# A hybrid decoder layer on one core: timed step lists against a list scheduler, and the middle down stages in two seven-product blocks

## The chip, the core and the metric

The kernel runs on one core of a Trainium2 chip. The metric is device time in microseconds (us) for one execution; smaller is better. Three runs of the kernel before gave 1723.19, 1723.62 and 1724.95 us, so its median is 1723.62 us.

## The reference

One decoder layer over 256 tokens of width 2048, all in float32:

```python
x = x + 0.5 * swiglu_ffn(rms_norm(x, ffn1_norm), w_gate, w_up, w_down)   # 2048 -> 5632 -> 2048
z = rms_norm(x, mix_norm) @ w_in
...
x = x + y @ w_out
x = x + 0.5 * swiglu_ffn(rms_norm(x, ffn2_norm), ...)
return rms_norm(x, final_norm)

def swiglu_ffn(x, w_gate, w_up, w_down):
    return (silu(x @ w_gate) * (x @ w_up)) @ w_down
```

The change touches the two feed-forward networks (FFN1 and FFN2, tags 1 and 2 in the kernel). The mixer between them (a gated recurrence and a short convolution) is left as it is.

## The kernel before

**Numbers in two parts.** Every float32 operand is split into a high part (rounded to the fp32r type, a cast on ScalarE) and a low part (the rest, a subtraction on VectorE). A product is three matmuls per block of 128 rows: high by high, low by high, high by low. A *unit* is 512 rows (four blocks) of a weight matrix by 512 columns, 1 MB: loading one issues a transfer on SyncE's queue into a *raw* tile, then two ScalarE casts of 1024 elements give the high part, then one VectorE subtraction of 2048 elements gives the low part, and both go to one of the *pair* tiles. One unit against 128 tokens is 4 x 3 = 12 matmuls, with the activations stationary and 512 weight columns moving. There are two token tiles (t = 0, 1) of 128 tokens.

**Seven products for eight.** `seven` (L471) takes two units of rows and two groups of columns as a 2 x 2 block matrix against two token tiles and two units of activations. Instead of eight unit products it makes seven, of sums and differences of weights (w11, w12, w21, w22, summed in place on VectorE and once by an accumulating transfer on GpSimd's queue) and of activations (`seven_of`). Products are named p0 to p6, banks of PSUM a, c, d, e. Other units of the same columns are multiplied plainly (x01, x11, x00, x10: unit 0 or 1, column group 1 or 0). Some banks are copied out in between ("snaps" s1, s5, u2, u3) and added at the end by VectorE.

**The stages of an FFN.** Hidden columns come in eleven units of 512. After the first unit and a first pair of seven-product blocks comes a *down* stage: the product of the hidden units that are there with their rows of `w_down`, all 2048 output columns (`down`, L884). Then, for s = 1 and s = 3, a *fine* stage of four seven-product blocks (gate, up, gate, up; two column groups each, so four hidden units) and again a down stage. The down stage after s = 1 has hidden units 3 to 6 and is called the middle one here; the one after s = 3 has units 7 to 10 and is the last. The row lists of the fine blocks hold five 128-row blocks per product (`tall`, L844) and three per plain unit (`short`): 7 x 15 + 4 x 18 = 177 matmuls per block.

**A down stage before.** `product` (L400) makes columns 0 plainly from four units, then `seven` makes columns 2 and 1 from the two newest units m, n as seven products and the two others plainly, then `product` makes columns 3. The newest hidden units are transposed on TensorE in `settle`/`turn_hidden` (L593 to 619); each gives a high part (ScalarE), a low part (VectorE), and for the middle stage also an exact copy (ScalarE) from which the sums for the seven products are made.

**What orders the work.** Inside a fine stage the order of every engine is written out by hand: `block` (L1036) holds a list of (time, step) pairs (L1109 to 1157), `fine_blocks` (L1163) shifts them by 40.2 us per block, sorts them and traces them in that order with `Engine.pinned` set, which ties each instruction behind the one traced before it on its engine. Down stages are not pinned: there the framework may issue an instruction earlier than its place in the text when its data are there. SyncE's queue is in order of the text. `prepare` (L1198) makes small vectors for the mixer: two transposes on TensorE (`turns`), copies of their results and some twenty tiny steps on VectorE, and two activations on ScalarE. Before, `down` calls it in the middle down stage of FFN1, ahead of `seven` (L955).

Of the kernel before, what the change touches and what calls it, by code (L numbers as in the profile page):

```python
# [16 lines left out]
P = 128  # L17
# [30 lines left out]

@with_exitstack
def hybrid_block(ctx: ExitStack, tc: tile.TileContext, a: dict, out: bass.AP):  # L50
# [30 lines left out]
    psum = ctx.enter_context(tc.tile_pool(name="psum", bufs=8, space=bass.MemoryType.PSUM))  # L81

# [97 lines left out]
    plan = deque()  # L180
    opened = []

    def pool_of(name, side, bufs=1):
# [3 lines left out]
        "three": (["pair0", "pair1", "pair2"], ["raw2", "raw1", "raw0", "kept", "spare"]),  # L187
# [4 lines left out]
    def open_stage(layout, raws=None):  # L192
# [3 lines left out]
        for side, names in (("left", left), ("right", right)):  # L196
            for name in names:
                pools[name] = pool_of(f"{name}_{n}", side, 2 if name in ("kept", "spare") else 1)
# [13 lines left out]

    def least_recent(kind):
        i = plan.popleft() if kind == "pair" and plan else recent[kind][0]
        recent[kind].remove(i)
        recent[kind].append(i)
        return f"{kind}{i}"

    def raw_tile(name, rows, role=None):
        if role in ("kept0", "kept1") and not fine():  # L220
            if extra:
                return bigs.tile([P, rows, CW], F32, tag="big", name=f"raw_{name}")
            return pools["kept"].tile([P, rows, CW], F32, tag="kept", name=f"raw_{name}", bufs=2)
# [353 lines left out]
    def ffn(tag, norm, after, opening=False):  # L577
        with tc.tile_pool(name=f"ffn{tag}", bufs=1, side="left", reuse_waits="tile") as fp:
# [14 lines left out]
            def turn_hidden(u, t, h, again):  # L593
# [4 lines left out]
                for j in range(UK):  # L598
                    pe.transpose(pt[:, j * P : (j + 1) * P], h[:, j * P : (j + 1) * P], ident)
# [284 lines left out]
            def down(last):  # L884
                us = sorted(set(hidden) | {w[0] for w in waiting})
                m, n = us[-2:]
# [22 lines left out]
                for c in (0, 3):  # L909
                    if c == 3:  # L910
                        plan.extend([1, 0, 1, 2][4 - len(us) :])
                    end = last and tag == 2 and c == NC_D - 1
                    ps = product(
                        wd, c, us[:-2] + [n, m], hidden.get, f"d{tag}_{m}_{c}", end,
# [9 lines left out]
                    if c == 0:  # L924
                        sh = {}
                        two, last_sum, high, low = seven_of(
# [28 lines left out]
                        if tag == 1 and m == 5:  # L955
                            prepare()
                        seven(
                            wd, (whole(m), whole(n)), (2 * CW, CW), sh, [of_unit(u, hidden[u]) for u in us[:-2]],
# [77 lines left out]
            def block(w, cs, name, b, done, gating, follows, handed):  # L1036

                raw, parts, bank_of, snaps, rest = {}, {}, {}, {}, {}
                home = {
                    "w11": (tall[0], 0, f"kept{b % 2}"), "w12": (tall[0], 1, f"kept{1 - b % 2}"),  # L1040
                    "w21": (tall[1], 0, "tall2"), "w22": (tall[1], 1, "tall1"),
                    "x01": (short[0][0], 1, "short0"), "x11": (short[1][0], 1, "short1"),
# [29 lines left out]
                def to(n):  # L1072
                    if n not in bank_of:
                        bank_of[n] = bank(f"ps_{name}_{n}")
# [607 lines left out]
```

## Time and profile before

| | us |
|---|---|
| median of three runs | 1723.62 |
| the profiled execution | 1727.47 |
| its span (first to last instruction) | 1725.5 |
| TensorE busy | 1708.7 |
| VectorE busy | 1506.8 |
| ScalarE busy | 1093.3 |
| fine stages of FFN1, from 200.76 and from 449.85 | 163.20, 163.60 |
| fine stages of FFN2, from 1211.64 and from 1462.44 | 165.33, 165.08 |
| middle down stages, from 363.96 and from 1376.97 | 85.89, 85.47 |
| last down stage of FFN2, from 1627.52 to the last matmul | 89.48 |

How to read it: in the profile PE is TensorE's matmul side, PEld its weight loads, DVE VectorE, ACT ScalarE, POOL GpSimd, SP SyncE. Nearly all instructions carry line L43, that of a helper that records them, so groups are told apart by the names of their tiles: `raw_d` is a raw tile of `w_down`, `hi_d_p` and `lo_d_p` the parts of a seven-product operand, `hi_d_x` those of a plain unit beside it, `hi_d` those of `product`; `g` and `u` stand for gate and up. A matmul's recorded duration overlaps the next one's, so the distance from one start to the next is its real price.

### The profile page before, as it was taken

To read this page: it belongs to the slowest core of one execution; us is meant where nothing else is said; L and a number is where in the kernel's file an instruction comes from. 1 tells how busy PE (TensorE), PEld (TensorE's weight loads), DVE (VectorE), ACT (ScalarE), POOL (GpSimd) and SP (SyncE) were. 2 spreads that over 40 slices of the span, in tenths; PEclk is the share of its full clock that TensorE was granted. 3 is DMA by queue.
4 is the path that set the end of the run, shared out by engine and by line. 5 is a ranking of instruction groups with operands and counts; after the bars stand their busy time and mean duration, and the time that the engine had idled before them with its cause. 6 is when DMAs were issued, how large, how long until landed. Compare 5 with 4: busy or idle time off the path is not lost.

```text
span 1725.5 us, 20385 instructions
## 1 busy us (share of the span) xinstructions
PE 1708.7 (99%) x7937; PEld 1424.3 (83%) x7937; DVE 1506.8 (87%) x1290; ACT 1093.3 (63%) x1344; POOL 45.7 (3%) x78
## 2 busy tenths in 40 slices
PE   9999999999999999999999999999999999999998
PEld 8888888888888888888888888888788888788876
DVE  7989899988799977887997888889899887899886
ACT  7766566655576666666866666655666654666654
POOL 0100000000000000000000000000000000000000
PEclk9999999999999999999999999999999999999999
DMA  8765877775887665655556574665977656877653
GB/s 304 234 222 179 270 236 233 227 236 167 263 269 224 202 224 193 222 190 176 173 194 225 190 266 149 219 226 186 300 240 226 213 173 239 258 232 238 231 165 122
DMA packets 181583, 376.78 MB, mean 218 GB/s; under 512 B 7412, under 2 KB 10352, under 8 KB 177776
## 3 DMA queue, kind: packets, MB, share of 16 engines
q1 hardware_dynamic: 174656, 340.81, 56.4%
q0 software_dynamic: 6656, 33.63, 10.4%
q8 instruction: 62, 1.02, 0.2%
q10 hardware_dynamic: 176, 1.06, 0.2%
q14 instruction: 33, 0.27, 0.0%
HBM read 339.82 MB, written 2.10 MB: 198 GB/s over the span
## 4 chain that ended last, share of the span: by engine, by line
PE 77%; issue 5%; DMA 5%; DVE 2%; ACT 1%; SPq 0%; POOL 0%; DVEq 0%; POOLq 0%; ACTq 0%
PE ps_in L43 10%; PE ps_u_a L43 9%; PE ps_d L43 8%; PE ps_g_a L43 8%; PE ps_u_c L43 6%; PE ps_g_c L43 4%; PE ps_u_d L43 4%; PE ps_g_d L43 4%; PE ps_d_a L43 4%; PE ps_o L43 3%; DMA raw_g_w<-raw_g_w 2%; PE ps_d_c L43 2%; PE ps_u_e L43 2%; PE ps_d_d L43 2%; PE ps_g_e L43 2%
## 5 line engine op out<-in xcount | busy, mean ns | idle before, releaser
L43 ACT CAST hi_g_p<-raw_g_w 128x1024 fp32r<-128x1024 f32 x112 | 137.9, 1262 | 69.5 <-PE ps_g_a L43 16.4
L43 ACT CAST hi_u_p<-raw_u_w 128x1024 fp32r<-128x1024 f32 x112 | 137.8, 1261 | 62.0 <-PE ps_u_a L43 20.9
L43 DVE TENSOR_TENSOR lo_g_p<-raw_g_w,hi_g_p 128x2560 fp32r<-128x2560 f32 (+2 forms) x72 | 158.5, 2225 | 20.5 <-PE ps_d L43 14.3
L43 DVE TENSOR_TENSOR lo_u_p<-raw_u_w,hi_u_p 128x2560 fp32r<-128x2560 f32 (+2 forms) x72 | 158.9, 2226 | 11.1 <-ACT hi_u_p L43 10.1
L43 PE MATMUL ps_d<-hi_d,h 128*128 128x512 f32 x696 | 166.1, 390 | 0.0
L43 PEld LDWEIGHTS ps_d<-hi_d,h 128*128 128x128 f32 x696 | 130.0, 188 | 26.7
L43 ACT CAST hi_d<-raw_d 128x1024 fp32r<-128x1024 f32 x88 | 87.4, 1047 | 72.5 <-PE ps_d_d L43 23.6
L43 PE MATMUL ps_in<-xT_nm,hi_in 128*128 128x512 f32 x512 | 122.5, 391 | 0.0
L43 DVE TENSOR_TENSOR lo_d<-raw_d,hi_d 128x2048 fp32r<-128x2048 f32 x44 | 99.7, 2288 | 23.8 <-ACT hi_d L43 23.7
L43 PEld LDWEIGHTS ps_in<-xT_nm,hi_in 128*128 128x128 f32 x512 | 94.0, 188 | 18.8 <-ACT tha L43 0.5
L43 ACT CAST hi_d_p<-raw_d 128x1024 fp32r<-128x1024 f32 x84 | 84.8, 1047 | 35.5 <-DVE raw_d L43 24.8
L43 DVE TENSOR_TENSOR lo_d_p<-raw_d,hi_d_p 128x2048 fp32r<-128x2048 f32 x42 | 95.0, 2284 | 7.4 <-ACT hi_d_p L43 7.4
L43 DVE TENSOR_TENSOR lo_in<-raw_in,hi_in 128x2048 fp32r<-128x2048 f32 x32 | 73.2, 2287 | 21.1 <-ACT hi_in L43 20.7
L43 PE MATMUL ps_d<-lo_d,h 128*128 128x512 f32 x348 | 86.2, 389 | 0.0
L43 ACT CAST hi_in<-raw_in 128x1024 fp32r<-128x1024 f32 x64 | 64.2, 1048 | 33.4 <-PE ps_in L43 18.0
L43 PEld LDWEIGHTS ps_d<-lo_d,h 128*128 128x128 f32 x348 | 65.3, 188 | 13.6
L43 DVE TENSOR_TENSOR raw_g_w<-raw_g_w,raw_g_w 128x1024 f32<-128x1024 f32 (+2 forms) x40 | 68.8, 1753 | 8.6 <-DMA raw_g_w<-in_ffn_w_gate_dram 8.2
L43 DVE TENSOR_TENSOR raw_u_w<-raw_u_w,raw_u_w 128x1024 f32<-128x1024 f32 (+2 forms) x40 | 68.8, 1753 | 0.6
L43 PEld LDWEIGHTS ps_in<-xT_nm,lo_in 128*128 128x128 f32 x512 | 65.6, 191 | 2.5
L43 PE MATMUL ps_in<-xT_nm,lo_in 128*128 128x256 f32 x512 | 66.4, 283 | 0.0
L43 ACT CAST hi_g_x<-raw_g_x 128x1536 fp32r<-128x1536 f32 x32 | 47.2, 1474 | 21.6 <-DMA raw_g_x<-in_ffn_w_gate_dram 20.3
L43 PE MATMUL ps_u_a<-hi_u_p,x 128*128 128x512 f32 x224 | 57.5, 393 | 0.0
(503 smaller groups left out, 3956.7 us busy)
## 6 DMA issues: line engine op xcount, KB each, us to landing
raw_d<-in_ffn_w_down_dram SPq DMA_DIRECT2D x88, 1024.0 KB, 5.2
raw_g_w<-in_ffn_w_gate_dram SPq DMA_DIRECT2D x32, 1024.0 KB, 5.8
raw_u_w<-in_ffn_w_up_dram SPq DMA_DIRECT2D x32, 1024.0 KB, 5.8
raw_in<-in_w_in_dram SPq DMA_DIRECT2D x32, 1024.0 KB, 5.0
raw_g_x<-in_ffn_w_gate_dram SPq DMA_DIRECT2D x32, 768.0 KB, 7.1
raw_u_x<-in_ffn_w_up_dram SPq DMA_DIRECT2D x32, 768.0 KB, 7.5
raw_u<-in_ffn_w_up_dram SPq DMA_DIRECT2D x23, 1024.0 KB, 5.4
raw_g<-in_ffn_w_gate_dram SPq DMA_DIRECT2D x22, 1024.0 KB, 5.2
```

Source lines behind the costliest of these rows:

```text
L43: ins = getattr(self.engine, name)(*args, **kwargs)
```

## The change

1. The hand-written step lists of the fine stages (`block`, `fine_blocks`) go. A class `Plan` takes steps with an engine, an assumed length, what they need and a tail; TensorE's order and the order of blocks are given, and `Plan.run` lays out VectorE, ScalarE, GpSimd and SyncE by earliest start and urgency, emitting each step as it is placed. Everything of a plan is traced pinned. Each stage has a plan of its own; the end state of one (when engines and tiles come free) is handed to the next.
2. Fine stages keep their blocks, products and tiles. Bank a is copied to bank d after p0 ("seed") and the products of d accumulate onto it; the snap s1 and its addition on VectorE go.
3. The middle down stage becomes two seven-product blocks, columns (2, 1) and (3, 0), both over the two *oldest* units p, q; the two newest are the plain units. One set of summed activations serves both blocks. The exact hidden values are made on VectorE as high plus low. The first block has a bank of its own for p4, and the sum of w11 and w21 for p3 is made by an accumulating transfer on GpSimd's queue, like that for p6.
4. The last down stage takes its two oldest units for the seven products, and makes their exact values on VectorE as well.
5. `prepare` is called between the plan of the middle down stage and that of the following fine stage.
6. Two extra raw tiles take the place of a pool of two; the four transposes of a hidden tile are one accumulation group.

The diff, cut to its core:

```diff
+    def turn_into(ps, sources):
+        for i, src in enumerate(sources):
+            pe.matmul(
+                ps[:, i * P : (i + 1) * P], src, ident, is_transpose=True, start=i == 0, stop=True,
+                skip_group_check=True,
+            )
...
+class Plan:
...
+    def run(self):
+        self.urgency()
+        order = {"PE": list(self.turn), "SP": sorted((z for z in self.steps if z.engine == "SP"), key=lambda z: z.late)}
...
+            for engine, steps in todo.items():
+                ripe = [(self.start_of(z), z) for z in steps if all(n.end is not None for n in z.needs)]
+                if ripe:
+                    soon = min(b for b, z in ripe) + 0.15
+                    found.append(min(((b, z) for b, z in ripe if b <= soon), key=lambda bz: bz[1].late))
...
+            self.free[step.engine] = begin + step.length
+            step.end = begin + step.length + step.tail + 0.07
...
             def down(last):
-                m, n = us[-2:]
+                m, n = us[-2:] if turned else us[:2]
+                rest = [u for u in us if u not in (m, n)]
...
+                        for u in () if turned else (m, n):
+                            for t in range(NT):
+                                turned[u, t] = quad(keep(f"hv{tag}_{u}_{t}"))
...
+                                dve.tensor_tensor(turned[u, t], hi, lo, op=ALU.add)
...
-            def block(w, cs, name, b, done, gating, follows, handed):
...
-                steps = [
-                    (-8.6, lambda: high("p0", two, three)), (-6.1, lambda: low("p0")),
...
+            step_mm, step_turn, add_sb, add_ps, copy_ps = 0.2267, 0.45, 0.6, 0.68, 0.6
+            def act_time(n):
+                return 0.2 + 0.425 * n
...
+            def dve_time(n):
+                return 0.06 + 0.554 * n
...
+                def by_transfer(key, other, *needs):
+                    z = plan.add("POOL", 1.0 + five, lambda: moved(key, other), *needs, tail=8.5)
...
+                        made["t1"] = by_pieces("w11", "w12", [made["p0"].lo[-1]])
+                        made["t3"] = by_transfer("w12", "w22", made["t1"][-1], loads["w22"])
...
+                        if turned4:
+                            sources = [by_transfer("w11", "w21", last, loads["w21"])]
...
+                    if q == 0:
+                        made["seed"] = plan.add("ACT", copy_ps, lambda: act.copy(to("d")(), to("a")()), u.low)
+                    elif q == 4 and apart:
+                        made["f"] = to("f"), u.low
...
+            def down_stage(s, free, ready, tails, later):
...
+                e21, e22 = exact(1, p), exact(1, q)
+                s4 = sum_step(of(1, q), of(1, p), of(1, q), ALU.subtract, e21, e22)
...
+                orders = [list(usual_order), usual_order[:8] + ["p3", "p1", "x10"]]
+                orders[0] = ["x01", lambda: turn_cells(plan, cells, turned), "p0", "x11", "p4", "p1", "p5", "p6", "x00", "p2", "p3", "x10"]
+                for i, cols in enumerate(((2 * CW, CW), (3 * CW, 0))):
...
             first_blocks()
             fifth()
+            handed = down(False)
...
             for s in (1, 3):
-                handed = down(False)
...
-                fine_blocks(s, handed)
+                done, tails, later = fine_stage(s, free, ready, handed)
...
+                if s == 1:
+                    done, handed = down_stage(s + 1, free, ready, tails, later)
+                    free, ready = settled(done, "three", "fine")
+                    hidden.clear()
+                    if tag == 1:
+                        prepare()
...
-            down(True)
+                    down(True)
```

More of the change, by code (lines that the diff above doesn't have):

```diff
@@ L597, in turn_hidden @@
                 pt = bank(f"ph{tag}_{u}_{t}")
[L598 to L599 removed]
+                turn_into(pt, [h[:, j * P : (j + 1) * P] for j in range(UK)])
                 pt = pt.rearrange("p (j c) -> p j c", j=UK)
```

642 lines of the change are left out of this document (510 added, 132 removed).

## The prediction, made before the changed kernel ran

> **What bounds the kernel now.** I first read the busy lines of the page, then a table of windows, one row per stage. Its columns are the stretch, its length, and the busy time of PE, PEld, DVE, ACT and POOL, each with its number of instructions, then the granted clock, the DMA share and GB/s.
>
> ```profile
> span 1725.5 us, 20385 instructions
> PE 1708.7 (99%) x7937; PEld 1424.3 (83%) x7937; DVE 1506.8 (87%) x1290; ACT 1093.3 (63%) x1344; POOL 45.7 (3%) x78
> ```
> ```profile
> 200.76:363.96 163.20, 163.20 (x734) 135.37 (x732) 152.86 (x100) 105.02 (x103) 6.28 (x8) 1.00 0.76 239
> 363.96:449.85 85.89, 85.89 (x384) 70.80 (x383) 70.08 (x67) 48.30 (x56) 0.86 (x1) 1.00 0.61 204
> 449.85:613.45 163.60, 163.49 (x733) 135.29 (x732) 153.03 (x100) 106.11 (x104) 7.04 (x8) 1.00 0.77 240
> 1211.64:1376.97 165.33, 163.50 (x733) 135.29 (x732) 153.85 (x100) 106.62 (x104) 7.01 (x8) 1.00 0.76 242
> 1376.97:1462.44 85.47, 85.47 (x381) 70.59 (x380) 67.87 (x47) 46.79 (x53) 0.86 (x1) 1.00 0.61 205
> 1462.44:1627.52 165.08, 163.52 (x734) 135.29 (x732) 152.86 (x100) 104.86 (x103) 7.03 (x8) 1.00 0.76 238
> 1627.52:1717.00 89.48, 87.62 (x393) 72.24 (x391) 69.85 (x67) 48.91 (x69) 0.89 (x1) 0.98 0.47 158
> ```
>
> TensorE is busy without a break in the middle down stages and nearly so in the fine ones. Busy alone does not show that it runs at its own pace, so I took the distance between starts, from the timeline of TensorE at the end of the FFN2 middle down stage:
>
> ```profile
> 1457.00 3.79 PE L43 MATMUL ps_d<-hi_d,h 128*128 128x512 f32 x16
> 1460.63 1.98 PE L43 MATMUL ps_d<-lo_d,h 128*128 128x512 f32 x8
> 1462.44 2.43 PE L43 MATMUL ps_g_a<-hi_g_p,x 128*128 128x512 f32 x10
> ```
>
> 24 matmuls go from 1457.00 to 1462.44: 0.2267 us each. A fine stage has 4 x 177 = 708 of them, 160.5 us, and six hidden tiles to transpose; 163.20 is what the first takes, so the hand-written order already leaves nothing in it. What there is to recover in the touched stages stands in three rows, whose bracket is TensorE's idle time before them:
>
> ```profile
> 1230.63 0.96 PE L43 MATMUL ps_g_e<-lo_g_x,x 128*128 128x512 f32 x3 [1.83 <-DVE lo_g_x L43]
> 1481.16 0.97 PE L43 MATMUL ps_g_e<-lo_g_x,x 128*128 128x512 f32 x3 [1.56 <-DVE lo_g_x L43]
> 1665.21 1.21 PE L43 MATMUL ps_d_a<-lo_d_p,hs 128*128 128x512 f32 x4 [1.82 <-DVE lo_d_p L43]
> ```
>
> All three end on a low part by VectorE: twice in the first block of a fine stage and once in the last down stage. So matmul count sets the time, and VectorE is close behind it (152.86 of 163.20, 94%).
>
> **The change, part by part.** *Matmuls.* A middle down stage before: two plain column groups, 2 x 4 units x 2 token tiles x 12 = 192 matmuls, and one seven-product block, 7 x 12 + 2 x 2 x 2 x 12 = 180; together 372. After: two such blocks, 360. Twelve matmuls fewer at 0.2267 is 2.72 us per FFN, **5.44 us** for both, and TensorE is full there, so it comes off the end. The eight transposes of the stage stay, as do all products of the fine and last stages. The seed copy replaces a snap on ScalarE, one for one.
>
> *VectorE in the middle down stage.* Its groups in the FFN2 stage now, and two rows that show its pace back to back:
>
> ```profile
> L43 DVE TENSOR_TENSOR lo_d_p<-raw_d,hi_d_p 128x2048 fp32r<-128x2048 f32 x7 | 15.8, 2285 | 1.8 <-ACT hi_d_p L43 1.8
> L43 DVE TENSOR_TENSOR lo_d<-raw_d,hi_d 128x2048 fp32r<-128x2048 f32 x7 | 15.8, 2288 | 2.7 <-ACT hi_d L43 2.5
> L43 DVE TENSOR_TENSOR raw_d<-raw_d,raw_d 128x2048 f32<-128x2048 f32 x3 | 6.9, 2285 | 0.0
> ```
> ```profile
> 1629.05 6.69 DVE L43 TENSOR_TENSOR lo_d<-raw_d,hi_d 128x2048 fp32r<-128x2048 f32 x3
> 1635.66 1.28 DVE L43 TENSOR_TENSOR h<-ph,h 128x512 fp32r<-128x512 f32 x2
> ```
>
> Three lows in 6.69 are 2.2 us apart, two 512-wide steps in 1.28 are 0.6 apart. After the change: 22 lows (eleven per block) 48.4 us; the in-place sums t1 and t2 of both blocks, 4 x 2.28 = 9.1 in halves; and 30 steps 512 wide (4 exact values, 4 activation sums, 4 lows of these, 4 lows of new hidden tiles, 2 gate tails, 12 updates of the residual) 18.0. That is 75.5 us, against 360 x 0.2267 plus 1.1 for the rest of the stage (85.47 - 372 x 0.2267), 82.7 us of TensorE: 91%, where it is 67.87 of 85.47 (79%) now. In fine stages it falls by four additions, 2.4 us, as s1 goes. So VectorE stays covered on average; where it does not, at the start of a stage, the cost is TensorE's wait. The second low of a stage is what is late next. I bound what such waits cost over the touched stages from minus 5.2 (the three above gone) to plus 9 us (a start at every one of the six stages as bad as 1.5), and take **0**: as many as now, since each stage is planned by itself and is no better informed about the next stage's first steps.
>
> *Transfers.* p3's sum goes to GpSimd's queue, so a middle down stage issues four accumulating transfers where it issued one; its weight loads stay sixteen.
>
> ```profile
> raw_d<-raw_d POOLq DMA_DIRECT2D x6, 1024.0 KB, 7.0
> q1 hardware_dynamic: 174656, 340.81, 56.4%
> q0 software_dynamic: 6656, 33.63, 10.4%
> ```
>
> q0's 33.63 MB hold 10.4% of the span, 5.3 us of all 16 engines per MB, q1's loads 2.85 per MB. A block's 8.4 MB of loads and 2.1 MB of sums make 24 + 11 = 35 of 41 us: 86% where the stage shows 0.61, and a fine stage 0.76. The transfer is 7.0 us median, and in the order given p6, p2 and x00 (10.9 us of matmuls) stand between p5, which frees w11, and p3. On SyncE, loads that wait for a raw tile hold up all loads behind them. I cost it at 0; if loads come late the bound is a wait of 2 us per block, 8 us in all.
>
> *Exact values on VectorE in the last down stage.* Four steps of 0.6 us per FFN, 4.8 in all; four ScalarE copies go. They read hidden units that are ready before the stage, so idle VectorE time hides them (69.85 of 89.48 busy); without cover the cost is 2.4 us in each. I take 0.
>
> *`prepare` between two plans.* A pinned step stands behind the step traced before it on its engine, so the fine stage's first VectorE and ScalarE steps now stand behind `prepare`'s last ones, and these need its transposes. Queued behind them are p0's casts and low, the sum t1, and p4's operands: all that the next stage starts with.
>
> ```profile
> 386.64 0.23 PE L43 MATMUL pv_many<-ident,rows_many 80*128 80x80 f32 x1
> 388.20 0.23 DVE L43 COPY cols_many<-pv_many 128x80 f32<-128x80 f32 x1
> 388.69 1.28 ACT L43 ACT_TABLE_LOAD   x1
> 389.99 0.21 ACT L43 ACTIVATE lam_exp<-lam_abs 128x8 f32<-128x8 f32 x1
> ```
> ```profile
> L122 POOL DMA_DIRECT2D rows_many<-in_sc_out_norm_dram x1: 508/508/508, 86.3 to 86.3; - x1
> ```
> ```profile
> 439.16 2.43 ACT L43 CAST hi_g_p<-raw_g_w 128x1024 fp32r<-128x1024 f32 x2 [3.36 <-PE ps_d L43]
> ...
> 442.85 2.83 DVE L43 TENSOR_TENSOR lo_g_p<-raw_g_w,hi_g_p 128x2560 fp32r<-128x2560 f32 x1 [4.42 <-PE ps_d L43]
> ...
> 449.85 2.43 PE L43 MATMUL ps_g_a<-hi_g_p,x 128*128 128x512 f32 x10
> 450.19 2.88 DVE L43 TENSOR_TENSOR lo_g_p<-raw_g_w,hi_g_p 128x1024 fp32r<-128x1024 f32 x2
> ...
> 455.51 1.07 PE L43 MATMUL ps_g_c<-lo_g_p,xs 128*128 128x512 f32 x4
> ```
>
> The transposes' rows were issued at 86.3 us, yet they ran at 386.64, where the text has them; they could run earlier than that only in a moment in which TensorE is held to have nothing else. If they slip into block two of the new stage, the cost is the two transposes, 0.4 us. If they stay at the boundary, it is a stall (third rival). No row shows this boundary, so both ends stand; I take the low one because the transposes are tied to nothing in front of them.
>
> **Sum.** Minus 5.44, and 0 for the rest. The profiled execution took 1727.47 us (span 1725.5), 3.85 above the median of the runs; its own forecast is 1722.0, and 1723.62 - 5.44 = **1718.2 us** for the median.
>
> **The rivals.** 0.2% of the time, 3.4 us, is about what a measurement of this kernel can tell from no change, so the lines are 1720.2 and 1727.1.
>
> 1. *The plan takes the gain back in waits.* The new down stage runs VectorE at 91% and DMA at 86%, and each boundary costs what 1230.63 shows. Four blocks at 1 to 2 us lose 4 to 8: 1720.2 to 1727. For it: the three waits now all end on VectorE. Against it: fine stages hold 94% without a wait inside. Chance 0.24.
> 2. *The old waits go.* With operands of the last stage from units long finished, the wait at 1665.21 vanishes, and with it a slow clock:
>
> ```profile
> 1666.00:1670.00 4.00, 4.00 (x12) 3.11 (x11) 4.00 (x3) 1.72 (x3) 0.00 (x0) 0.57 0.19 72
> ```
>
> 12 matmuls start in 4 us there where 17.6 fit: 1.3 us more. Minus 5.44 - 1.82 - 1.3 gives 1715.1; with both fine starts clean too, 1711.7. Chance of under 1715.5: 0.10.
> 3. *Slower: `prepare` holds the boundary of FFN1.* Let T be the end of the middle stage's matmuls. Copy 0.45 us after the transpose, and from the copy (388.20) to the end of lam_exp (390.20) 2.0 us: ScalarE resumes at T + 2.5, p0's casts end at T + 4.9 (2.43), and p0's low starts there. Now it starts at 442.85, 7.0 us before TensorE's 449.85. VectorE is late by 11.9; of that about 2 us is slack (p4's low ends at 453.07 and is wanted at 455.51), so 10 us are lost, and at 94% load it can't give back a lead that TensorE has already waited for. 1718.2 + 10 = 1728.2. It decides from 8.9 us on. Chance 0.24.
>
> A rule of the Trainium skill speaks against the change here: "TensorE: Matmul & The Clock Gate", Part 1, says that an idle window of about 3.4 us sets the matmul clock to half until it has been busy for about as long again. The row above shows the half clock after an idle time of only 1.82 us, while 1.83 and 1.56 us left the rows around them at 1.00: the price agrees with the rule, the threshold does not. By it the third rival's time would be an estimated 1730.
>
> That the change does not do what it says would show as 372 matmuls in the stage; it is in no case above.
>
> **How the numbers follow.** Forecast 1718.2, with its own range 1715.5 to 1720.2: 0.42. Rival 1: 0.24, rival 2: 0.10, rival 3: 0.24. Faster 0.42 + 0.10 = 0.52, within 0.2% 0.24, slower 0.24. The range goes from 1714.0 (half of rival 2 left out) to 1729.0 (over rival 3's 1728.2, short of its tail): about 0.15 is left out.
>
> **What would show it.** Right: middle down stages of about 82.7 us with 360 products, no idle time on TensorE over 2 us, fine stages at 163 to 165. Rival 1: brackets on TensorE inside the down stage naming `lo_d`, or DMA `raw_d` ahead of casts. Rival 2: no half clock near the end. Rival 3: `pv_many` at the last matmul of FFN1's middle stage, VectorE idle for some 8 us before it, and TensorE idle for some 10 us behind it. The prediction is wrong if stalls elsewhere exceed 9 us, or if untouched stages move.

## The result, and the profile after

The changed kernel takes 1748.23 us (median of 4 runs, 1747.63 to 1751.64) beside 1724.28 for the kernel before on the same chip: ratio 1.0137, 95% interval 1.0114 to 1.0161, slower by some 24 us. The forecast was 1718.2 and the third rival's time 1728.2. The profiled execution of after took 1748.15 us.

The page of after, its span and busy lines:

```profile
span 1746.4 us, 20389 instructions
PE 1715.0 (98%) x7913; PEld 1420.4 (81%) x7913; DVE 1530.6 (88%) x1320; ACT 1096.0 (63%) x1346; POOL 50.8 (3%) x84
```

There are 24 matmuls fewer (7913 records for 7937), and yet the span is 20.9 us longer. The table of stages of after (columns as in the prediction): FFN1's middle down stage and the fine stage behind it; FFN2's first blocks, first, middle and last down stage.

```profile
365.96:456.02 90.06, 84.39 (x372) 68.13 (x370) 71.56 (x66) 49.28 (x59) 3.48 (x4) 1.00 0.76 222
456.02:627.40 171.38, 166.93 (x732) 136.08 (x733) 164.55 (x119) 109.84 (x106) 7.02 (x8) 0.99 0.73 231
1077.04:1165.44 88.40, 85.63 (x378) 70.15 (x376) 69.83 (x49) 50.48 (x61) 0.86 (x1) 0.98 0.67 213
1165.44:1235.16 69.72, 65.72 (x286) 53.58 (x284) 58.57 (x44) 38.56 (x44) 1.54 (x3) 0.98 0.58 191
1399.26:1485.56 86.30, 84.16 (x370) 67.87 (x368) 76.75 (x62) 50.27 (x58) 3.45 (x4) 1.00 0.74 220
1650.95:1737.98 87.03, 86.14 (x393) 71.10 (x391) 67.36 (x62) 47.08 (x66) 0.86 (x1) 1.00 0.48 158
```

The two of before that the prediction had no need of, FFN2's first blocks and first down stage:

```profile
1063.97:1147.92 83.95, 83.76 (x377) 69.15 (x376) 69.84 (x49) 50.07 (x60) 0.86 (x1) 1.00 0.67 219
1147.92:1211.64 63.72, 63.72 (x285) 52.49 (x284) 57.33 (x43) 38.42 (x45) 0.86 (x1) 1.00 0.60 199
```

Length against length: FFN1's middle stage plus 4.2 and its second fine stage plus 7.8; FFN2's first blocks plus 4.5 and first down stage plus 6.0. These four make 22.4 us. FFN2's middle stage is 0.8 longer in place of 2.7 shorter, its last stage 2.4 shorter. The causes lie in three places.

**A. The boundary behind FFN1's middle stage.** The timeline of after, all engines:

```profile
452.75 0.23 PE L43 MATMUL pv_many<-ident,rows_many 80*128 80x80 f32 x1
...
453.02 0.24 DVE L43 COPY cols_many<-pv_many 128x80 f32<-128x80 f32 x1 [6.82 <-PE pv_many L43]
...
453.30 0.21 ACT L43 ACTIVATE lam_abs<-cols_many 128x8 f32<-128x8 f32 x1 [11.06 <-DVE cols_many L43]
...
456.02 4.14 PE L43 MATMUL ps_g_a<-hi_g_p,x 128*128 128x512 f32 x10 [2.83 <-ACT hi_g_p L43]
...
458.02 2.83 DVE L43 TENSOR_TENSOR lo_g_p<-raw_g_w,hi_g_p 128x2560 fp32r<-128x2560 f32 x1
```

This is the third rival's mechanism: `pv_many` stands at the stage's last matmul, VectorE is idle for 6.82 us and ScalarE for 11.06 us until its result comes, and p0's low stands behind all of `prepare`. Only TensorE's share looks different: not some 10 us of idle time in one piece, but 2.83 us, then 4.14 us for ten matmuls where 2.27 is its pace, then shorter waits (0.74, 0.96, 0.85 and 1.48 us up to 471.69).

**B. Raw tiles of the unplanned stages.** In FFN2's first blocks, which begin 13.07 us later in after, two loads of the up block leave SyncE's queue at the same moments of the stage in both kernels, but not for the same tiles. What waits for a load shows which it is. In the kernel before, w11's load leaves at 1077.94, early enough that the first cast of the up block waits for a pair tile alone (PE is its releaser), and w12's at 1095.99. SyncE and that cast in the kernel before:

```profile
1077.94 0.37 SPq L43 DMA_DIRECT2D raw_u<-in_ffn_w_up_dram  x1
```
```profile
1096.81 1.05 ACT L43 CAST hi_u_p<-raw_u 128x1024 fp32r<-128x1024 f32 x1 [1.33 <-PE ps_g_a L43]
```

In after the two have changed places: w12's load leaves at 1091.01 (1077.94 plus 13.07), and w11's, which is wanted first, at 1109.06 (1095.99 plus 13.07). It lands at 1115.85, and the first cast of the up block stands for it:

```profile
1109.06 0.37 SPq L43 DMA_DIRECT2D raw_u<-in_ffn_w_up_dram  x1
```
```profile
1115.95 1.05 ACT L43 CAST hi_u_p<-raw_u 128x1024 fp32r<-128x1024 f32 x1 [7.40 <-DMA raw_u<-in_ffn_w_up_dram]
```

With a pool of two, the next block's w11 takes the buffer of the last block's w12, which is read last by p6: the load at 1077.94 leaves as p6's low ends (1077.93). With a tile for each, it waits for the last block's w11, which p3 reads at the very end: the load at 1109.06 leaves as p3's low ends (1109.03). These blocks are not pinned, and SyncE's queue does not keep the order of the text here, as "The kernel before" has it: the load at 1077.94 leaves ahead of the gate block's last one, at 1082.61. Then, in the last column group of the first down stage, a unit put by hand on `raw3`, the fixed tile of w11, comes late as well. Its load leaves at 1210.67, as p3's low there ends (1210.65), and lands at 1215.99 (TensorE of after):

```profile
1217.12 5.51 PE L43 MATMUL ps_d<-hi_d,h 128*128 128x512 f32 x16 [4.00 <-ACT hi_d L43]
```

**C. Inside the planned middle stages.** FFN2's takes 86.30 us for the 82.7 worked out, 3.6 more. For 2.14 us of it TensorE is idle (86.30 less 84.16), in three waits (three stretches of the timeline of TensorE, after):

```profile
1423.19 2.11 PE L43 MATMUL ps_d_a<-hi_d_p,hs 128*128 128x512 f32 x8 [0.73 <-ACT u_d L43]
```
```profile
1436.86 0.50 PE L43 MATMUL ps_d_a<-lo_d_p,h 128*128 128x512 f32 x1 [0.68 <-DVE lo_d_p L43]
```
```profile
1479.06 1.20 PE L43 MATMUL ps_d_d<-lo_d_p,h 128*128 128x512 f32 x4 [0.73 <-DVE lo_d_p L43]
```

The first is p6 right behind p5 on bank a, waiting for the snap between them; the others are the low parts of p3 and p1. Both of these lows are late behind a load. In the second block ScalarE waits for a plain unit's raw tile, VectorE for the cast of it, and from there VectorE's lows follow one another up to p1's (ScalarE and VectorE of after):

```profile
1466.87 2.00 ACT L43 CAST hi_d_x<-raw_d_x 128x1024 fp32r<-128x1024 f32 x2 [8.04 <-DMA raw_d_x<-in_ffn_w_down_dram]
```
```profile
1468.90 2.29 DVE L43 TENSOR_TENSOR lo_d_x<-raw_d_x,hi_d_x 128x2048 fp32r<-128x2048 f32 x1 [6.06 <-ACT hi_d_x L43]
```

The load had left at 1457.30 and landed at 1466.78. In the first block ScalarE waits 3.17 us for such a load (issued at 1423.01), and VectorE 2.80 us for the cast behind it, just ahead of p3's low.

### The profile page after: what moved, and what is told of

Same layout as the page of the kernel before. It is cut to its first block, busy times and chain, and to the rows that moved or that the text cites. A ratio compares the mean times of both kernels' runs of the same rounds, so it can differ in the third digit from the quotient of the medians.

```text
span 1746.4 us, 20389 instructions
## 1 busy us (share of the span) xinstructions
PE 1715.0 (98%) x7913; PEld 1420.4 (81%) x7913; DVE 1530.6 (88%) x1320; ACT 1096.0 (63%) x1346; POOL 50.8 (3%) x84
## 5 line engine op out<-in xcount | busy, mean ns | idle before, releaser
L43 PE MATMUL ps_d<-hi_d,h 128*128 128x512 f32 x440 | 107.0, 396 | 5.0 <-ACT hi_d L43 5.0
L43 PEld LDWEIGHTS ps_d<-hi_d,h 128*128 128x128 f32 x440 | 83.1, 190 | 22.9 <-ACT hi_d L43 5.8
L43 ACT CAST hi_d<-raw_d 128x1024 fp32r<-128x1024 f32 x56 | 55.5, 1046 | 40.9 <-PE ps_d_d L43 11.5
L43 ACT CAST hi_d_p<-raw_d 128x1024 fp32r<-128x1024 f32 x56 | 56.4, 1046 | 31.6 <-DVE raw_d L43 16.8
L43 DVE TENSOR_TENSOR lo_d_p<-raw_d,hi_d_p 128x2048 fp32r<-128x2048 f32 x28 | 63.4, 2285 | 10.9 <-ACT hi_d_p L43 10.7
L43 DVE TENSOR_TENSOR lo_d<-raw_d,hi_d 128x2048 fp32r<-128x2048 f32 x28 | 63.6, 2287 | 9.4 <-ACT hi_d L43 9.3
L43 DVE TENSOR_TENSOR lo_d_p<-raw_d_w,hi_d_p 128x2048 fp32r<-128x2048 f32 (+1 forms) x36 | 64.7, 1812 | 6.7 <-ACT hi_d_p L43 6.7
L43 ACT CAST hi_d_p<-raw_d_w 128x1024 fp32r<-128x1024 f32 x56 | 56.9, 1047 | 18.5 <-DVE raw_d_w L43 9.3
L43 PE MATMUL ps_g_a<-hi_g_p,x 128*128 128x512 f32 x224 | 58.3, 398 | 2.8 <-ACT hi_g_p L43 2.8
```

Of the source, the lines that this page charges most:

```text
L43: ins = getattr(self.engine, name)(*args, **kwargs)
```

## The experiments

The theory is that A, B and C are separate and add up, and that the two-block stage itself is worth its 24 product matmuls. The first rival is that the pinned plan loses wherever it meets other code, so that undoing one place moves the wait to the next. Each ratio is to runs of the kernel before on the same chip beside it, with its 95% interval.

**`prepare` in the last down stage of FFN1** (A undone):

```diff
-                    if tag == 1:
-                        prepare()
...
-                        if tag == 1 and m == 5:
+                        if tag == 1 and last:
                             prepare()
```

> Only the place of prepare is changed: it is called in the last down stage of FFN1, ahead of the seven-product block, and no longer between the two plans. Theory 1 (prepare holds VectorE and ScalarE at the boundary until TensorE has run its transposes): the waits of TensorE from the boundary to 473 us go, about 10.7 us with the half-clock window in them, so about 1737.5 us and a fine stage of FFN1 that takes 164 to 165 us like that of FFN2. Rival (the planned order is late at that boundary by itself): only the 3 us right at the boundary go, about 1745.

It takes 1740.29 us, ratio 1.0098 (1.0083 to 1.0113). The fine stage behind the boundary:

```profile
451.90:616.78 164.88, 164.01 (x733) 135.18 (x732) 157.12 (x105) 106.32 (x103) 7.02 (x8) 1.00 0.77 248
```

It is back from 171.38 to 164.88 and the middle stage from 90.06 to 86.67: 9.9 us in the traces, 7.9 in the medians, nearer to the theory's time than to the rival's. A is a cause by itself.

**The pool of two again** (B undone; the plan's stage keeps its two extra tiles):

```diff
-        "three": (..., ["raw2", "raw1", "raw0", "raw4", "raw3", "spare"]),
+        "three": (..., ["raw2", "raw1", "raw0", "kept", "spare"]),
+        "planned": (..., ["raw2", "raw1", "raw0", "raw4", "raw3", "spare"]),
...
-            return pools["raw3" if role == "kept0" else "raw4"].tile(...)
+            return pools["kept"].tile(..., bufs=2)
...
-                        if len(us) == 3:
-                            chosen["raw"].extend([3] + [i for i in recent["raw"] if i in (1, 2)])
```

> Only the raw tiles of the stages that are not planned go back to what they were: one pool of two tiles for w11 and w12 in place of a fixed tile for each, and no chosen order of raw tiles for columns 3 of the first down stage; the planned down stage keeps its five tiles. Theory 1 (a fixed tile for w11 is free only after p3's low, so SyncE's queue stands still and the next block's loads come late): the 4.5 us in FFN2's first blocks, the 6.0 in its first down stage and 0.9 in FFN1's go, about 1737 us. Rival (those stages lose because their neighbours are planned, or because of the order the framework finds): they stay long and the time stays at 1746 to 1749.

It takes 1740.94 us, ratio 1.0103 (1.0088 to 1.0118). FFN2's first blocks, first down stage and first fine stage:

```profile
1077.59:1161.78 84.19, 83.74 (x377) 69.17 (x376) 69.85 (x49) 50.29 (x61) 0.86 (x1) 1.00 0.70 221
1161.78:1225.34 63.56, 63.56 (x285) 52.65 (x284) 53.24 (x40) 36.25 (x42) 0.89 (x1) 1.00 0.55 175
1225.34:1392.83 167.49, 164.96 (x733) 134.84 (x732) 159.19 (x105) 107.78 (x104) 7.04 (x8) 1.00 0.78 251
```

The first two are as before again (10.4 us less); the third takes 3.4 back (164.10 in after). A smaller edit tells why: only the two lines with `chosen["raw"]`, which pick raw tiles from a list, are left out.

> The changed kernel without the one line that picks raw tiles for the last column group of the first down stage (3, then 1 and 2); the two fixed raw tiles stay. If that line makes the first down stages late, FFN2's goes from 69.72 to about 64 us and FFN1's from 65.30 to 64.4, 1748 - 6.5 = 1741.5, the first blocks of FFN2 staying at 88.4. Rival: the fixed tiles in the first blocks put SyncE's queue behind, and the down stage inherits that: 66 us or more there, 1745 to 1748.

It takes 1746.49 us, ratio 1.0120 (1.0105 to 1.0135). FFN2's first down stage and first fine stage:

```profile
1164.54:1228.40 63.86, 63.86 (x285) 52.35 (x284) 53.67 (x40) 36.15 (x42) 0.89 (x1) 1.00 0.53 171
1228.40:1396.07 167.67, 165.16 (x734) 134.85 (x732) 158.66 (x104) 107.34 (x104) 7.02 (x8) 1.00 0.77 249
```

The list alone made the first down stage late, as expected (69.72 to 63.86), and the fixed tiles the first blocks: these stay at 87.18 without the list. But the list had bought something too: the fine stage behind is 3.6 us longer without it. The theories of both texts were right on their stages and missed the next one.

**Both undone:**

> Both edits: prepare in the last down stage, and the old pool of raw tiles in the stages that are not planned. If the two causes are separate their gains add: about 1748.2 - 10.7 - 11 = 1726.5 us, and what is left over 1724.3 - 5.4 is the waits inside the planned stages, about 7. Rival (one wait only uncovers another): 1732 or more.

It takes 1730.59 us, ratio 1.0045 (1.0029 to 1.0061). By the medians over the kernel before beside each, after is 23.95 us slower, A undone 17.18, B undone 17.83 and both undone 7.48: that is 6.8 and 6.1 us apart and 16.5 together. So one does not take the other's gain away; why the two together give more than their sum, if it is more than noise, no run here shows. The time lies between the two that were expected. What is left is C and the late fine stage of FFN2.

**A alone, without a planner:** the kernel before, with `prepare` called behind the middle down stage.

```diff
-                        if tag == 1 and m == 5:
-                            prepare()
...
                 handed = down(False)
+                if tag == 1 and s == 3:
+                    prepare()
```

> The kernel before, with nothing changed but the place of prepare: called after the middle down stage of FFN1, ahead of the hand-written fine stage, as the change does. Theory 1: the fine stage's first VectorE and ScalarE steps are tied behind prepare's last ones there too, so TensorE loses about 10 us at that boundary: about 1734 us. Rival (the loss needs the planner): the framework moves prepare ahead in a stage that is not pinned, and the time stays within 2 us of 1724.3.

It takes 1733.25 us, ratio 1.0059 (1.0042 to 1.0075), 10.1 us over the kernel before beside it. Its timeline at the boundary:

```profile
448.87 0.23 PE L43 MATMUL pv_many<-ident,rows_many 80*128 80x80 f32 x1
...
449.14 0.24 DVE L43 COPY cols_many<-pv_many 128x80 f32<-128x80 f32 x1 [11.69 <-PE pv_many L43]
...
452.13 4.15 PE L43 MATMUL ps_g_a<-hi_g_p,x 128*128 128x512 f32 x10 [2.83 <-ACT hi_g_p L43]
```

These are the same rows with hand-written lists and an unpinned down stage. The transposes did not slip in earlier, though their rows had been issued at 86.3, some 360 us before. The price belongs to the place of the call.

**C: two places in TensorE's given order** (on top of both repairs):

```diff
-                orders = [list(usual_order), usual_order[:8] + ["p3", "p1", "x10"]]
-                orders[0] = [..., "p4", "p1", "p5", "p6", "x00", "p2", "p3", "x10"]
+                orders = [list(usual_order), list(usual_order)]
+                orders[0] = [..., "p4", "p5", "p1", "p6", "x00", "p2", "p3", "x10"]
```

> The changed kernel with both repairs (prepare late, pool of two), and two steps moved in TensorE's given order of the middle down stage: p1 between p5 and p6 of the first block, so that the snap of bank a is covered, and x10 ahead of p1 in the second. If the planned stage's waits are places in that given order, 0.89 + 0.93 us go per FFN: 1730.6 - 3.6 = 1727 us, middle stages of 84 to 85.5 us. Rival: VectorE is late by its load, so the waits turn up at the next low part: 1730 to 1731, stages of 86 to 87.5.

It takes 1728.76 us, ratio 1.0025 (1.0016 to 1.0035). The middle stage and the next fine stage of FFN1, then FFN2's first fine and middle stages:

```profile
366.24:449.50 83.26, 83.03 (x369) 68.27 (x368) 73.20 (x58) 48.92 (x56) 3.48 (x4) 1.00 0.73 211
449.50:616.67 167.17, 164.68 (x733) 134.91 (x732) 159.37 (x107) 107.55 (x104) 7.03 (x8) 1.00 0.76 245
1216.15:1383.46 167.31, 164.83 (x733) 134.93 (x732) 158.78 (x104) 107.68 (x104) 7.04 (x8) 1.00 0.77 250
1383.46:1466.95 83.49, 83.25 (x369) 68.14 (x368) 74.40 (x60) 48.95 (x56) 3.45 (x4) 1.00 0.74 215
```

The middle stages are now what the prediction had worked out, 82.7 us, within 0.8: TensorE is idle for 0.23 and 0.24 us, with VectorE at 88 and 89%. So C was in the order, not in the amount of work. The load of the first block's last plain unit now leaves at 1407.19 and nothing waits for it; that the order does this by freeing raw tiles at other moments is read from the trace, and no run changes it alone. FFN1's fine stage behind gives 2.8 us back (164.40 with both repairs only). A part of this is work that moved: VectorE does 73.20 us in FFN1's middle stage, where it did 76.41 with both repairs only, and the rest comes behind the stage's end.

**The late fine stage of FFN2.** Its first load leaves SyncE's queue at 1206.31, 9.8 us ahead of the stage; that of FFN1's first fine stage leaves at 185.38, 17.1 us ahead of 202.51. SyncE there, and VectorE just before:

```profile
1206.31 0.92 SPq L43 DMA_DIRECT2D raw_g_w<-in_ffn_w_gate_dram  x2
```
```profile
1203.99 2.29 DVE L43 TENSOR_TENSOR lo_d<-raw_d,hi_d 128x2048 fp32r<-128x2048 f32 x1 [0.92 <-ACT hi_d L43]
```

The load goes as the last low of the down stage ends (1206.28): it waits for that unit's raw tile. In FFN1 the turns of the tiles end on other ones. The next kernel turns them by one ahead of FFN2's first blocks:

```diff
+            if tag == 2:
+                recent["raw"].insert(1, recent["raw"].popleft())
             first_blocks()
```

> The previous repaired kernel (prepare late, pool of two, p1 between p5 and p6, x10 ahead of p1), and in FFN2 the order in which the three raw tiles take turns is turned by one ahead of its first blocks, so that the first down stage ends on the tiles that the plan of the next fine stage assumes (in FFN1 it does already). If a load that stands in SyncE's queue for the last raw tile makes FFN2's first fine stage late (its first load is issued 9.8 us ahead of the stage, FFN1's 17.1), that stage goes from 167.31 to about 164 us: 1728.8 - 3.3 = 1725.5. Rival: VectorE is late there in any case, 167 us, 1728 to 1729.

It takes 1726.31 us, ratio 1.0009 (0.9998 to 1.0020). FFN2's first fine stage:

```profile
1214.47:1378.21 163.74, 163.74 (x733) 135.22 (x732) 154.27 (x101) 105.47 (x103) 6.39 (x8) 1.00 0.77 242
```

The stage is 3.6 us shorter, as expected, and its first load leaves 17.2 us ahead of it (1197.25). The whole is level with the kernel before.

**How the middle stage ends.** Here are two more orders of its second block, on top of that:

```diff
-                orders = [list(usual_order), list(usual_order)]
+                orders = [list(usual_order), usual_order[:8] + ["p3", "p1", "x10"]]
```

> The kernel with the turned raw tiles, and the second block of the middle down stage in the change's own order again (p3, p1, x10). If a stage that ends on a plain unit (5.44 us of matmuls for one low part) gives VectorE its lead into the next stage, and one that ends on products (2.72 us each) does not, the wait in the stage comes back (0.93 us each) and FFN1's second fine stage falls from 167.2 to 164.5: 1725.5 - 1 = 1724.5. Rival: the end of the stage doesn't matter, the wait of 0.93 is simply added: 1727.

```diff
-                orders = [list(usual_order), list(usual_order)]
+                orders = [list(usual_order), usual_order[:7] + ["p1", "x00", "p3", "x10"]]
```

> The kernel with the turned raw tiles, and the second block ordered p1, x00, p3, x10 behind p2, so that it ends on a plain unit without p1's low part being late. By the same theory both the wait in the stage and the one behind it go: middle stages of 83.3 to 83.6 and second fine stages of 164 to 165 us, 1722 to 1723, as fast as the kernel before. Rival: p6, p2 and p1 in a row (8.2 us of matmuls) outrun VectorE, which needs 2.28 us for each low part besides the updates: 1 to 2 us per stage lost there, 1725 to 1727.

The first takes **1721.29 us, ratio 0.9980 (0.9971 to 0.9989): the only kernel here that beats the one before.** The second takes 1727.18 us, ratio 1.0013 (1.0004 to 1.0022). The fine stages behind the two middle stages, in the first:

```profile
450.05:616.45 166.40, 164.63 (x733) 135.02 (x732) 156.32 (x105) 106.06 (x103) 7.02 (x8) 1.00 0.74 239
1462.42:1627.70 165.28, 164.67 (x734) 134.99 (x733) 156.95 (x106) 105.91 (x103) 7.02 (x8) 1.00 0.75 240
```

They had 167.62 and 167.16 with p1 at the end; the middle stages gave back 0.8 and 0.3 (84.05 and 83.57). That is 2.1 us in these traces and 5.0 in the medians; the profiled execution of the faster kernel is the slowest of its eleven runs (1725.43), so its trace doesn't show where the rest lies. The second block of this kernel has the change's own order again, and in FFN2 ScalarE still waits 6.87 us there for a plain unit's load (1443.75), but TensorE is idle for 0.24 us in the whole stage. So most of C goes with the place of p1 in the first block alone, and this late load costs TensorE next to nothing there. In the other order the waits that its rival named are there (TensorE):

```profile
434.33 2.15 PE L43 MATMUL ps_d_d<-hi_d_p,h 128*128 128x512 f32 x8 [1.37 <-ACT hi_d_p L43]
437.91 1.19 PE L43 MATMUL ps_d_d<-lo_d_p,h 128*128 128x512 f32 x4 [1.44 <-DVE lo_d_p L43]
```

Its middle stages take 86.73 and 85.96 us, and yet the fine stages behind them 165.69 and 164.93, near the 164 to 165 that its text had: the end on a plain unit does give VectorE its lead, and the price lies inside the stage.

The first rival of this section is thus half right. Two repairs gave something back in the next stage (3.4 us behind B's, 2.8 behind C's), but the kernel came from 1748.23 to 1721.29 us in all, with the plans still in it. Of the 5.44 us that were counted, it then has 3.9 under the kernel before beside it (1725.19).

**The two blocks without a plan.** This is the kernel before with only its middle stage changed and its order left to the framework; a second kernel takes the oldest units in the last stage as well.

```diff
-                handed = down(False)
+                handed = two_blocks() if s == 3 else down(False)
```

`two_blocks` holds x01, the transposes, p0, x11, p4, p5, p2, p6, x00, p3, x10, p1 for columns 2 and 1, then calls `seven` for columns 3 and 0 with the same summed activations.

> The kernel before with its hand-written fine stages, its first and its last down stages; only the middle down stage becomes two seven-product blocks over the two oldest units, as in the change, with no plan and nothing pinned (the framework orders it), exact values on VectorE, p4 of the first block in a bank of its own, p2 between p5 and p6, p3's sum on VectorE, the small vectors made ahead of the second block. If the waits of the planned middle stages (3.3 to 3.8 us each) belong to the plan and not to the two blocks, the 12 products saved per FFN come off the end: middle stages of about 83 us with 360 products, 1724 - 5.4 = 1718 us (1716.5 to 1720). Rival: two blocks with VectorE at 91% wait for low parts whoever orders them: 85 us and more per stage, 1722 to 1725.

> The previous one, and the last down stage with its two oldest units for the seven products and their exact values on VectorE, as the change has it. If the last stage's wait of 1.82 us and the slow matmuls behind it (1.3 us) are there in every execution of the kernel before, 2 to 3 us less than the previous kernel, some 1715.5. Rival: they come and go (another profile of the kernel before's own last stage had 87.58 us where the first had 89.39, and after has 87.03): 0.5 us less, within 1 us of the previous kernel.

They take 1744.07 us (ratio 1.0103, 1.0086 to 1.0119) and 1746.01 us (1.0121, 1.0106 to 1.0136). The theories of both texts fell; the first one's rival of 1722 to 1725 was far too low as well. (The 87.58 in the second text is from the run with the moved `prepare`, whose FFN2 is that of the kernel before.) The last stage took 87.33 us in the second kernel, where kernels with the old one have 87.6 to 89.6: no gain that a time shows. The middle and second fine stages of FFN1 in the first:

```profile
364.44:453.07 88.63, 85.16 (x372) 67.85 (x370) 75.93 (x70) 48.86 (x58) 1.72 (x2) 1.00 0.60 193
453.07:622.64 169.57, 166.49 (x733) 135.89 (x733) 159.84 (x103) 110.79 (x107) 7.04 (x8) 0.99 0.77 239
```

The middle stages are longer here than in the kernel before (88.63 and, in FFN2, 90.71 for 85.89 and 85.47), with twelve product matmuls fewer in each: TensorE waits in them for casts `hi_d_p`, 1.74 us at 385.47 and 2.58 at 1408.82. The runs below go after the fine stages. One theory for these: the stage ends on products, 2.72 us of matmuls for each low part, in place of plain units, 5.44 us. So p1 was put ahead of the last x10:

> The hand-written kernel with two blocks in the middle down stage (1744.07), and in the second of them p1 ahead of x10, so that the stage ends on a plain unit as the kernel before's does; nothing else moves. If the hand-written fine stages behind it are late (6.45 and 6.63 us) because the stage ends on products, VectorE gets its lead back: second fine stages of 169.6 and 169.8 fall to some 166, 1744 - 7 = 1737 (1735 to 1740). Rival: the lead is lost by the work in the whole stage (22 low parts and 30 small steps on VectorE), not by its end: the fine stages stay at 169 to 170, 1743 to 1745.

It takes 1742.18 us, ratio 1.0102 (1.0085 to 1.0119); the fine stages stayed at 169.6. That theory fell. The time is near its rival's 1743 to 1745, but the trace names another cause (ScalarE):

```profile
452.32 1.04 ACT L43 CAST hi_g_p<-raw_g_w 128x1024 fp32r<-128x1024 f32 x1 [10.68 <-PE ps_d_d L43]
```

ScalarE stands 10.68 us until the stage's last product frees a pair tile. The kernel before and the plan pick the pairs of the last units; my `two_blocks` took them in turn. With the plan's list:

```diff
+                plan.extend([0, 1, 2] * 5 + [0, 1, 2, 1, 0, 1, 2])
```

> The hand-ordered two-block kernel that ends on a plain unit (1742.2), with the pair tiles of the middle stage picked so that the last unit has the third one (the change's own list). If ScalarE's wait of 10.68 us for a pair tile made the fine stages behind it late, its cast moves ahead of the stage's end: second fine stages of 169.6 become 164 to 165, and the 1.29 us at the boundary goes: 1742.2 - 11 = 1731 (1729 to 1733). Rival: VectorE has no lead in a two-block stage in any case, 167 us and more, 1736 to 1740.

> The same with the stage ending on the product p1 in place of the plain unit x10. If the end of the stage sets VectorE's lead (in the planned kernels the plain end gave 5 us of the median), 2 to 5 us more than the previous kernel: 1733 to 1736. Rival: only the pair tile mattered here, within 1 us of the previous kernel.

> The first of these with the planned kernels' order in the first block: p4, p5, p1, p6, x00, p2, p3, x10 in place of p4, p5, p2, p6, x00, p3, x10, p1. If the waits in its middle stage (1.9 and 0.7 us ahead of p5 in FFN1, 1.7, 0.7 and 0.7 in FFN2) come from p2's and p6's operands being made too soon, 2.5 to 3 us less per stage: 1731 - 5.5 = 1725.5, as fast as the kernel before or just behind. Rival: VectorE is behind at p5 by its load in the stage's first 20 us, whatever follows p5: 1730 to 1732.

They take 1741.30, 1738.69 and 1737.94 us (ratios 1.0092, 1.0083 and 1.0080; all intervals within 1.0067 to 1.0106). All three forecasts were too low, by 3 to 12 us, and none of the rivals' times came out either; whether the stage ends on x10 or on p1 makes no difference here that the intervals can tell. The cast came earlier, but another instruction took the wait over (VectorE of the first of the three):

```profile
454.46 0.69 DVE L43 SCALAR_TENSOR_TENSOR xres<-ps_d_a,xres 128x512 f32<-128x512 f32 x1 [5.44 <-PE ps_d_a L43]
455.06 2.82 DVE L43 TENSOR_TENSOR lo_g_p<-raw_g_w,hi_g_p 128x2560 fp32r<-128x2560 f32 x1
```

An update of the residual needs the last unit's bank and stands ahead of the next stage's first low, whose cast was done. The kernel before and the changed one both hand the last two updates into the next stage; `two_blocks` handed one. With both handed over:

```diff
-                    if (t, b) == (0, 0):
+                    if b == 0:
                         handed.append(z)
```

> The hand-ordered two-block kernel with picked pairs and the plan's order of the first block (1737.9), with both last updates of the stage handed over into the next stage, as the kernel before does, in place of one. If that update held VectorE's queue (idle 4.58 us ahead of it, the next stage's first low part behind it), the second fine stages fall from 168.1 to 164: 1737.9 - 8 = 1730 (1728 to 1732). Rival: without the plan the stage leaves VectorE no lead; 166 us and more, 1734 to 1738.

> The same hand-over in the kernel with picked pairs that ends on p1 and has p2 between p5 and p6 (1738.7; VectorE idle 2.70 us at the stage's end). By the same theory second fine stages of 167.3 and 166.4 fall to 164 to 165: 1738.7 - 5 = 1733.5. Rival: no change, 1737 to 1739.

They take 1738.29 and 1738.59 us (ratios 1.0083, 1.0070 to 1.0095, and 1.0086, 1.0072 to 1.0100): nothing is gained, as both rivals had it. The low came early (449.45), and ScalarE then waited for a load (the first of the two kernels):

```profile
457.20 1.47 ACT L43 CAST hi_g_x<-raw_g_x 128x1536 fp32r<-128x1536 f32 x1 [7.78 <-DMA raw_g_x<-in_ffn_w_gate_dram]
```

Pair tile, update, load: each wait removed showed the next one behind it, and the time stayed between 1738 and 1742 us. What SyncE's queue waits for there stands in the same trace:

```profile
447.94 0.37 SPq L43 DMA_DIRECT2D raw_g_w<-in_ffn_w_gate_dram  x1
```

The next stage's third load, and all behind it, leave only as a low of the down stage ends (447.92) and frees a raw tile, 5.2 us ahead of the stage at 453.19. In the kernel before, the stage's third load leaves at 438.46, 11.4 us ahead of 449.85. In the kernel here TensorE stands 2.92 us for a cast at 459.68, behind the one in the row above. So a raw tile's turn is the likely cause that is left, as in B and in FFN2's late fine stage; no run changed it here.

## Why the prediction was wrong, point by point

- **Matmuls: right.** There are 360 product matmuls in a middle stage, 24 fewer in the two, at 0.2267 us each. With C out of the way these stages take 83.26 and 83.49 us for the 82.7 worked out. VectorE's work there was sized well too (76.75 us for 75.5).
- **`prepare`: the failed step.** Of the two ends, 0.4 and some 10 us, the prediction took the low one "because the transposes are tied to nothing in front of them". They ran at the stage's last matmul, in after and in the kernel before with the call moved, with VectorE's and ScalarE's first steps of the next stage behind them. The high end was right: 9.9 us in the traces, 10.1 in the hand-written kernel. The row that should have decided was quoted: rows issued at 86.3, transposes at 386.64, where the text had them. The third rival, with 0.24, had the mechanism, the place and the price; its 1728.2 fell short of 1748.23 because the terms below came on top, and the some 10 us of TensorE were not one idle time but 2.83 us, slow matmuls and shorter waits.
- **Raw tiles: a missing term.** Point 6 of the change had no line in the sum. FFN2's first blocks and first down stage, of which the prediction said nothing, lost 10.4 us. "If untouched stages move" was the condition given for being wrong, and it came true.
- **Waits in the planned stages and transfers: both sized 0, measured 3.6 us over in FFN2's middle stage** (2.14 of it idle), and 4.0 in FFN1's once `prepare` is moved (86.67). VectorE at 91% was not by itself the cause: it stands idle for 2.80 and 6.06 us there. What it stood idle for was a load that came late ahead of a cast, which the prediction's signs name ("DMA `raw_d` ahead of casts"); ScalarE waits 8.04 us for one in the row above. The share of DMA was 0.74 to 0.76 in these stages, not 86%. Another place for p1 in the first block took most of these 3.6 us away; which part of them is the loads' and which the order's own, the runs don't tell.
- **The old waits: partly.** In the last stage the half clock is gone (1.00 in the table above), but runs of kernels with the old stage have 87.6 as well as 89.4 us, so that the 1.82 us were not a steady price. In FFN2's fine stages the waits of 1.83 and 1.56 us are gone too (164.10 and 165.39 us, 0.03 and 0.74 of it idle), but FFN2 of the kernel before, in the run with the moved `prepare`, has 163.87 and 164.72 as well.
- **VectorE in fine stages: wrong.** The 2.4 us fewer did not come: FFN2's first has 153.97 us of VectorE for 153.85. The four additions are gone, but exact values for the next down stage are made there.
- **Exact values on VectorE in the last stage: right at 0.** The stage takes 87.03 us in after and 87.33 in the two-block kernel with the oldest units in its last stage, under the 87.6 to 89.6 of the old one.
- The range ended at 1729.0, 0.8 above the third rival's time. Rival 3 and a part of rival 1 together already gave more than that; they were taken as alternatives, and they add up.

## What to carry to other kernels

When a change lays out queues by a plan, look first at what the plan does not hold: a call between two plans, and a tile whose turn changes in stages that the plan never sees. Ask of each which in-order queue stands behind it; here these two were some 17 of the 24 us, while the counted work of the middle stages came out within 1 us. Busy shares do not show a load that leaves late; look at when each stage's loads leave, and at what frees their tiles. A saving of products in a stage also takes its slack at the end: the next stage's first operands need their tiles, their casts and their loads before it ends, and each of these can be the one that is late.

## What the runs showed of the hardware

The half clock came after shorter waits than the rule cited below has it. After 2.83 us of idle TensorE (456.02, above) ten matmuls took 4.14 us. The window over them, and one behind an idle time of 2.58 us in the two-block kernel:

```profile
456.02:460.16 4.14, 4.14 (x10) 2.90 (x10) 3.80 (x12) 1.32 (x1) 0.00 (x0) 0.59 1.00 370
```
```profile
1408.82:1411.40 2.58, 2.58 (x6) 2.10 (x7) 2.58 (x2) 0.89 (x1) 0.00 (x0) 0.50 1.01 340
```

The waits of 1.37 and 1.44 us quoted above left the rows behind them nearly at pace (eight matmuls in 2.15, four in 1.19; without a wait 1.98 and 1.07). "TensorE: Matmul & The Clock Gate", Part 1, of the Trainium skill puts the idle window at about 3.4 us; these rows have the half clock after less, and 1.82 and 1.83 us in the prediction went either way, so one idle time alone doesn't decide it here. The price of the 2.83 us is that wait and about 1.9 us more (4.14 less 10 at 0.2267).
